# Two more Strassen pairs for the ZA gate blocks of a three-branch mixer, with their gate applied after the read-back

## The chip, the cores and the metric

The kernel runs on one core of one Trainium2 chip. The metric is the device time of one execution in microseconds (us). Three executions of the kernel before took 877.57, 877.92 and 880.95 us; the median is 877.92. One further execution was profiled.

The engines are named as in the profile: PE is TensorE (matmuls), PEld its weight loads, DVE is VectorE, ACT is ScalarE, POOL is GpSimd, SP is the engine from which nearly all DMAs are issued, in order.

## The reference

One decoder layer on a sequence of 1024 tokens with 1024 channels, in float32. Cut to what matters:

```python
mod = c @ w_ada + b_ada
shift, scale, gate = split(mod, 3)
h = rms_norm(x, g_pre) * (1 + scale) + shift
proj = h @ w_in
q_a, kv_c, kv_s, kv_w, g_nsa, z_a, q_b, kv_b, z_b, merge = split(proj)
# mixer A: 8 heads of 64, 2 key/value groups, three branches
o_a = g0 * compressed(q_a) + g1 * selected(q_a) + g2 * windowed(q_a)
y_a = (merge_heads(o_a) * silu(z_a)) @ w_o_nsa
# mixer B: 8 heads, a window of 128 with sinks
o_b = banded_attention(q_b, k_b, v_b, window=128, sinks)
y_b = (merge_heads(o_b) * silu(z_b)) @ w_o_swa
m_a, m_b = split(merge, 2)
y = (sigmoid(m_a) * y_a + sigmoid(m_b) * y_b) @ w_out
out = x + gate * rms_norm(y, g_post)
```

With 16 selected blocks out of 16, the selected branch is full causal attention. `z_a` and `z_b` are 512 columns each, `m_a` and `m_b` 1024 each.

## The kernel before

**Numbers in two halves.** Every float32 operand of a large product is split into a high part (a cast to float32r) and a low part (the rest). A product of a 128-column weight block and a 512-token half is then high x high + high x low + low x high. Over the 8 channel blocks of 128 this makes 24 matmuls of 128x512; over half of them, 12. Splitting a weight quarter (128x512) costs an ACT cast (`wh`) and a POOL subtraction (`wl`), in `split_half` (L180, L183). The input `h` lies in SBUF as `hh` and `hl`, 8 channel blocks x 2 token halves.

**Strassen pairs.** Two weight blocks of 128 columns x two channel halves x two token halves are a 2x2x2 block product. Instead of 8 half products of 12 matmuls each, a pair takes 7 (Winograd's form): two on raw weight quarters of the first block and the raw input half 0 (`raw_products`), three with sums of weights S2, S1, S4, of which two use the input sums T2 and T1 (`middle_products`), and two with S3 on T3 and a quarter of the second block on T4 (`last_products`). The weight sums S1 to S4 are formed on POOL from the four quarters, four additions a pair, and stored to DRAM (`pair_sums`, L852). The input sums T1 to T4 are formed in `input_sums` on POOL and stored; later `set_load` loads one of them over four pairs of `hh` and `hl` tiles whose contents are no longer needed, and `set_form` splits it (an ACT cast L1161, a POOL subtraction L1162, four times each). Partial results go through DRAM: x after the first raw product, then u and e. Before the change the 8 pairs are the 16 merge blocks MA0 to MA7 and MB0 to MB7. The gate blocks ZA0 to ZA3 and ZB0 to ZB3 are plain products of 24 matmuls for each token half.

**Stages.** (1) Norm, conditioning and first projections, to about 95 us. (2) The compression MLP of mixer A, with the gate blocks ZB0 to ZB3, ZA0, ZA1 in between, in 24 steps of 12 matmuls (`z_steps`); `input_sums` hangs on the same steps. (3) Two units of attention of mixer B, one for each key/value group, and then two units of mixer A, each over 8 query tiles of 128. (4) A seam of the last four pairs' last products, then the projection of mixer B by `w_o` with the preparation of `w_out`, that of mixer A, and the output product, itself in seven products.

**What sets the order.** Within the attention, each tile's scores go PE, DVE (masked add with a running minimum, L980), ACT (exponential), DVE (reciprocal), POOL (scaling by the reciprocal and gate, L1002), then PE transposes (L1039), an ACT cast and a DVE subtraction, and PE products with V. Between them stand the projections of the next heads, and pieces of the products of the pairs. In the A units these are written as a `line` of parts: part n of a line stands at the share n / len(line) of the unit's ideal PE time. `pieces` are pumped in that order; a piece may not come before the PE instruction that stands AHEAD of it, and PE work that stands LAG behind it may not come before it. In the B units late gate products run whole at even distances (`Late`, four of them). Weight sums are pieces too, from `late_sums` (B units) and `paced_sums` (A units). Inside these bounds a list scheduler orders each engine's instructions at compile time; each engine then runs its own in order.

**Buffers that matter.** Raw weight quarters have 3 buffers (`wraw`), split ones 6 each. The tag `kt` has 6 tiles of 128x512 and holds partial results, gate temporaries and some keys; `pj` has 2 of 8 PSUM banks. In the last stage the heads are read back through 3 buffers (`t1`).

**The gate of mixer A.** `z_out` makes z * (1 + tanh(z / 2)), twice the SiLU, and stores it to DRAM. `finish` (L1067) loads the gate for a finished query tile as two small DMAs, multiplies the tile by it on POOL, and stores it to `o_dram` (L1070). `heads_out` loads the heads again by halves (L1423), casts on ACT (L1424) and subtracts on DVE (L1425). Before the change heads 4 to 7 (mixer B) are read at the start of the seam, and 0 to 3 after blocks 1, 3, 5, 7 of the projection of mixer B, where `sums_b` also splits the rows of `w_out` (L1495).

## Time and profile before

| what | value |
|---|---|
| median of three executions | 877.92 us |
| profiled execution | 879.03 us |
| its span, first to last instruction | 877.3 us |
| mean granted TensorE clock | 0.993 |
| PE busy | 861.1 us (98%), 4406 matmuls |
| DVE / ACT / POOL busy | 619.0 / 535.1 / 544.0 us |
| DMA | 155.93 MB, mean 178 GB/s |

A row of the groups view names line, engine, operation, output <- inputs, shapes and count, then busy us and mean ns of one, then the engine's idle time before them and what ended most of it. A row of the waits view says who waited for whom: us in total, times, longest us. A row of the stages view has the stretch, its length, and for each engine the busy us with the count of instructions, then the granted clock, the DMA engines' share and GB/s. A row of a timeline has start, length, the instruction, a count where neighbours are merged, and in brackets the idle time before it. A row of the view of one line or tile has the shortest, median and longest duration in ns, then the first and last start.

### The profile page before, as it was taken

To read this page: it belongs to the slowest core of one execution; us is meant where nothing else is said; L and a number is where in the kernel's file an instruction comes from. 1 tells how busy PE (TensorE), PEld (TensorE's weight loads), DVE (VectorE), ACT (ScalarE), POOL (GpSimd) and SP (SyncE) were. 2 spreads that over 40 slices of the span, in tenths; PEclk is the share of its full clock that TensorE was granted. 3 is DMA by queue.
4 is the path that set the end of the run, shared out by engine and by line. 5 is a ranking of instruction groups with operands and counts; after the bars stand their busy time and mean duration, and the time that the engine had idled before them with its cause. 6 is when DMAs were issued, how large, how long until landed. Compare 5 with 4: busy or idle time off the path is not lost.

```text
span 877.3 us, 14795 instructions
## 1 busy us (share of the span) xinstructions
PE 861.1 (98%) x4406; PEld 726.4 (83%) x4406; DVE 619.0 (71%) x1592; ACT 535.1 (61%) x1222; POOL 544.0 (62%) x554
## 2 busy tenths in 40 slices
PE   8999999999999999999999999999999999999996
PEld 6989888888888878888888788888888788887885
DVE  4866677456666677776775677666685399779996
ACT  6466844277768787675776876665565465444341
POOL 2000786568879788987474977664574379646451
PEclk7999999999999999999999999999999999999999
DMA  9874688755545445674225443423554589741333
GB/s 346 287 281 157 223 280 275 255 176 183 150 145 169 136 134 157 213 233 164 75 70 186 124 133 109 145 90 127 196 176 133 180 317 305 283 130 40 108 103 113
DMA packets 95618, 155.93 MB, mean 178 GB/s; under 512 B 11057, under 2 KB 28849, under 8 KB 95538
## 3 DMA queue, kind: packets, MB, share of 16 engines
q1 hardware_dynamic: 89616, 144.84, 50.3%
q10 hardware_dynamic: 5922, 10.14, 3.7%
q8 instruction: 35, 0.57, 0.3%
q14 instruction: 45, 0.37, 0.1%
HBM read 111.43 MB, written 39.85 MB: 172 GB/s over the span
## 4 chain that ended last, share of the span: by engine, by line
PE 94%; DVE 2%; ACT 2%; DMA 1%; issue 1%; POOL 1%; SPq 0%; DVEq 0%; POOLq 0%; ACTq 0%
PE b_pt L1039 8%; PE b_pj L1106 7%; PE b_pj L1112 7%; PE b_pj L1111 7%; PE b_pv L1050 4%; PE b_s L973 4%; PE b_s L970 4%; PE b_pv L1047 4%; PE b_pj L213 3%; PE b_pj L206 3%; PE b_pj L214 3%; PE b_pj L594 1%; PE b_pj L586 1%; PE b_s L593 1%; PE b_s L586 1%; PE b_pj L593 1%
## 5 line engine op out<-in xcount | busy, mean ns | idle before, releaser
L183 POOL TENSOR_TENSOR wl<-wraw,wh 128x512 fp32r<-128x512 f32 x126 | 171.7, 1365 | 103.7 <-ACT wh L180 72.7
L1046 DVE TENSOR_TENSOR pl<-b_pt,ph 128x512 fp32r<-128x512 f32 x162 | 109.7, 686 | 45.1 <-ACT ph L1045 44.6
L1045 ACT CAST ph<-b_pt 128x512 fp32r<-128x512 f32 x162 | 93.1, 584 | 58.2 <-PE b_pt L1039 45.1
L180 ACT CAST wh<-wraw 128x512 fp32r<-128x512 f32 x118 | 72.5, 618 | 60.3 <-PE b_pj L1111 23.6
L993 ACT ACTIVATE ps<-ps,mins 128x257 f32<-128x257 f32 (+9 forms) x128 | 81.1, 635 | 29.2 <-DVE mins L980 27.6
L970 PE MATMUL b_s<-kh,q 128*128 128x256 f32 (+6 forms) x272 | 86.4, 324 | 1.3 <-DVE rr L997 1.1
L973 PE MATMUL b_s<-kl,q 128*128 128x256 f32 (+6 forms) x272 | 83.7, 314 | 0.0
L1002 POOL TENSOR_SCALAR ps<-ps,rr,gates 128x128 f32<-128x128 f32 (+7 forms) x64 | 52.8, 829 | 31.7 <-DVE rr L997 23.7
L1050 PE MATMUL b_pv<-pl,V 128*128 128x512 f32 x162 | 69.0, 426 | 1.2 <-DVE pl L1046 1.0
L1106 PE MATMUL b_pj<-hh,wh 128*128 128x512 f32 x168 | 68.6, 410 | 0.0
L1039 PE MATMUL b_pt<-ident,ps 128*128 128x128 f32 x408 | 67.9, 272 | 0.0
L1047 PE MATMUL b_pv<-ph,V 128*128 128x512 f32 x162 | 66.4, 410 | 1.4 <-ACT ph L1045 1.2
L1112 PE MATMUL b_pj<-hh,wl 128*128 128x512 f32 x168 | 66.4, 395 | 0.0
L1111 PE MATMUL b_pj<-hl,wh 128*128 128x512 f32 x168 | 66.2, 394 | 0.0
L1039 PEld LDWEIGHTS b_pt<-ident,ps 128*128 128x128 f32 x408 | 51.4, 140 | 10.3 <-DVE pl L1018 0.2
L970 PEld LDWEIGHTS b_s<-kh,q 128*128 128x128 f32 x272 | 51.2, 188 | 9.7 <-issue 1.7
L973 PEld LDWEIGHTS b_s<-kl,q 128*128 128x128 f32 x272 | 51.3, 189 | 6.8
L1002 POOL TENSOR_SCALAR pw<-pw,rr,gates 128x640 f32<-128x640 f32 (+4 forms) x64 | 47.6, 747 | 12.5 <-DVE rr L997 9.9
L993 ACT ACTIVATE pw<-pw,mins 128x640 f32<-128x640 f32 (+4 forms) x64 | 44.5, 696 | 13.5 <-DVE mins L980 12.6
L997 DVE RECIPROCAL rr<-sums 128x1 f32<-128x1 f32 x192 | 28.3, 158 | 24.1 <-ACT pw L993 12.6
L206 PE MATMUL b_pj<-hh,wh 128*128 128x512 f32 x112 | 44.6, 398 | 0.0
L213 PE MATMUL b_pj<-hl,wh 128*128 128x512 f32 x112 | 44.3, 396 | 0.0
(460 smaller groups left out, 2588.2 us busy)
## 6 DMA issues: line engine op xcount, KB each, us to landing
wraw<-in_w_blk SPq DMA_DIRECT2D x82, 256.0 KB, 3.3
wraw<-sS SPq DMA_DIRECT2D x32, 256.0 KB, 2.8
r<-in_w_out SPq DMA_DIRECT2D x32, 256.0 KB, 4.2
wa<-in_w_adaT SPq DMA_DIRECT2D x15, 512.0 KB, 5.0
w1raw<-in_w ACTq DMA_DIRECT2D x16, 256.0 KB, 3.2
gr<-in_w_adaT ACTq DMA_DIRECT2D x8, 512.0 KB, 7.1
wraw<-in_w_o SPq DMA_DIRECT2D x16, 256.0 KB, 4.5
t<-od SPq DMA_DIRECT2D x16, 256.0 KB, 4.5
```

What stands on the lines that cost most here:

```text
L183: chain("wl", nc.gpsimd.tensor_tensor(wl, raw, wh.bitcast(F32), ALU.subtract))
L970: ins = nc.tensor.matmul(sp[:, :n_in], lhsT=q, rhs=rh, start=True, stop=False)
L973: nc.tensor.matmul(sp[:, :n_in], lhsT=q, rhs=rl, start=False, stop=True)
L993: nc.scalar.activation(rows[r][:, :on], rows[r][:, :on], AF.Exp, scale=-1.0, bias=last_min[:, r : r + 1], accum_out=sums[:, r : r + 1])
L1002: nc.gpsimd.tensor_scalar(rows[r][:, :off], rows[r][:, :off], rr[:, r : r + 1], gate, ALU.mult, ALU.mult)
L1039: ins = nc.tensor.transpose(t[:, r * P : r * P + P], rows[r][:, off : off + P], ident)
L1046: nc.vector.tensor_tensor(pl, t, ph.bitcast(F32), ALU.subtract)
L1047: ins = nc.tensor.matmul(pv, lhsT=v, rhs=ph, start=(first and n == 0), stop=False)
L1050: nc.tensor.matmul(pv, lhsT=v, rhs=pl, start=False, stop=(last and n == len(todo) - 1))
L1106: ins = nc.tensor.matmul(self.t, lhsT=wh[:, kc, :], rhs=hi, start=(self.first is None and kc == 0), stop=False)
L1111: nc.tensor.matmul(self.t, lhsT=wh[:, kc, :], rhs=lo, start=False, stop=False)
L1112: ins = nc.tensor.matmul(self.t, lhsT=wl[:, kc, :], rhs=hi, start=False, stop=(kc == KH - 1 and self.stop))
```

## The change

- `PAIRS` gets two pairs in front, (ZA0, ZA1) and (ZA2, ZA3), so there are ten. `raw_ends` makes the two evacuations of a raw pair of products; `settle` applies z * (1 + tanh(z / 2)) where the block is a Z, and stores. These and `raw_half_product` serve all places below.
- The raw products are spread out: pairs 0 to 3 (ZA0, ZA2, MA0, MA2) beside the MLP in `z_steps`, after ZB0 to ZB3; pairs 4 to 7 as the four `Late` steps of the B units; pairs 8 and 9 in unit A of group 0.
- The weight sums: pairs 0, 1 and 2, 3 in the two B units, 4 to 7 in unit A of group 0, 8 and 9 in group 1.
- In group 0 the projections of group 1's first half are reordered so that channel half 1 is used up first (`parts` with order (1, 0), and `turned_products` for pair 9, whose sum is added on POOL); T2 and T1 are then loaded and formed there, and the middle products of pairs 0 to 3 run in group 0. Group 1 has those of pairs 4 to 9 and the last products of pairs 0 to 5. The seam keeps the last four pairs.
- `finish` no longer loads or multiplies a gate for mixer A. `heads_out` loads the gate for heads 0 to 3 and multiplies on POOL, 128x512 eight times. Heads 0 and 1 are read during the seam, 2 and 3 after blocks 1 and 3 of the projection of mixer B.

The diff, cut to its core:

```diff
-PLAIN = ["ZA2", "ZA3"]
-PAIRS = [(f"MA{2 * m}", f"MA{2 * m + 1}") for m in range(4)] + [(f"MB{m + 4}", f"MB{m}") for m in range(4)]
+PAIRS = [("ZA0", "ZA1"), ("ZA2", "ZA3")] + [(f"MA{2 * m}", f"MA{2 * m + 1}") for m in range(4)] + [(f"MB{m + 4}", f"MB{m}") for m in range(4)]
-FIRST = 3
+NRAW = (4, 4)
+SUMS = ((0, 1), (2, 3), (4, 5, 6, 7), (8, 9))
+NMID = 4
...
+    def settle(name, half, tile, th=None):
+        if name.startswith("Z"):
+            if th is None:
+                th = kq.tile([P, HS], F32, name="acc", tag="kt", bufs=6)
+            nc.scalar.activation(th, tile, AF.Tanh, scale=0.5)
+            nc.vector.scalar_tensor_tensor(tile, th, 1.0, tile, ALU.add, ALU.mult)
+        store(half_of(name, half), tile)
+
+    def raw_ends(p):
+        c = {}
+        def keep(t):
+            c["x"] = kq.tile([P, HS], F32, name="acc", tag="kt", bufs=6)
+            nc.scalar.copy(c["x"], t)
+            store(x_dram[p], c["x"])
+        def whole_(t):
+            sp = kq.tile([P, HS], F32, name="sp", tag="sp", bufs=1)
+            nc.vector.tensor_tensor(sp, c["x"], t, ALU.add)
+            settle(PAIRS[p][0], 0, sp, c["x"])
+        return keep, whole_
...
-        zs = z_steps([f"Z{m}{b}" for m, b in (("B", 0), ("B", 1), ("B", 2), ("B", 3), ("A", 0), ("A", 1))])
+        zs = z_steps([f"ZB{b}" for b in range(4)], range(NRAW[0]))
...
-        for p in range(2):
+        for p in range(2) if mixer == "B" else ():
             src = spilled[f"Z{mixer}{2 * g + p}"]
...
-        nc.gpsimd.tensor_tensor(ot, ot, zt.rearrange("d r t -> d (r t)"), ALU.mult)
+        if mixer == "B":
+            nc.gpsimd.tensor_tensor(ot, ot, zt.rearrange("d r t -> d (r t)"), ALU.mult)
...
         def whole(self):
-            if not self.w:
-                self.w.extend(load_block(self.name))
-            z_out(self.name, self.half, proj_half(self.w, self.half, lambda: bank("pj")))
+            w = load_block(PAIRS[self.p][0])
+            for j, end in enumerate(raw_ends(self.p)):
+                end(raw_half_product(self.p, j, w[j], lambda: bank("pj"))[0])
...
+    def turned_products(p):
...
+        def keep(t):
+            c["y"] = kq.tile([P, HS], F32, name="acc", tag="kt", bufs=6)
+            nc.scalar.copy(c["y"], t)
+        def whole_(t):
+            x = kq.tile([P, HS], F32, name="acc", tag="kt", bufs=6)
+            nc.scalar.copy(x, t)
+            store(x_dram[p], x)
+            nc.gpsimd.tensor_tensor(c["y"], c["y"], x, ALU.add)
+            store(half_of(a, 0), c["y"])
+        return (Part(Weights(quarter_of(a, 0)), h_set(0, 0), None, whole_),
+                Part(Weights(quarter_of(a, 1)), h_set(1, 0), None, keep))
...
-        late += [Late(name, half, w) for half in range(2)]
+    late = [Late(p) for p in range(NRAW[0], sum(NRAW))]
...
             if u == 2:
-                line = raw_products([0]) + plan_k(g, 1) + plan_q("A", g, 1)
-                line += raw_products([1, 2, 3, 4, 5]) + plan_k(1, 0) + plan_q("A", 1, 0) + raw_products([6, 7])
...
-                behind(line[-1], half_free)
+                rest = range(sum(NRAW), NP)
+                line = raw_products(rest[:1]) + plan_k(g, 1) + plan_q("A", g, 1)
+                q0, q1 = (parts(f"QA1{p}", [0], lambda name, half, t, p=p: q_block("A", 1, p, half, None, t), (1, 0))
+                          for p in range(2))
+                k1 = parts("KA1", [0], lambda name, half, t: k_block([("slc", 1), ("win", 1)], half, None, t), (1, 0))
+                z0, z1 = turned_products(rest[1])
+                line += q0 + [z1, q1[0], k1[0], q1[1], k1[1], z0]
+                behind(k1[0], lambda: set_load("T2", 1, 0))
+                behind(z0, lambda: set_load("T1", 0, 0))
+                mids = [middle_products(p, True) for p in range(NMID)]
+                at0 = len(line)
+                line += [m[0] for m in mids] + sum((m[1:] for m in mids), [])
+                for name, first in (("T2", at0 - 1.2), ("T1", at0 + 2)):
+                    for k in range(KH):
+                        pieces.append((begun + whole[u] * (first + 0.3 * k) / len(line),
+                                       lambda at, name=name, k=k: paced_form(name, k, at)))
+                for n, p in enumerate(SUMS[u]):
+                    for f, share in zip(paced_sums(p), (0.0, 0.05, 0.07, 0.09, 0.11)):
+                        pieces.append((begun + whole[u] * (share + 0.085 * n + 0.05), f))
             else:
                 line = plan_k(g, 1) + plan_q("A", g, 1)
                 behind(line[-1], lambda: set_load("T3", 0, 1))
-                for n, name, k in ((1, "T2", 0), (2, "T2", 1), (3, "T2", 2), (3, "T1", 0),
-                                   (4, "T2", 3), (4, "T1", 1), (5, "T1", 2), (5, "T1", 3)):
-                    ahead_of(line[n], lambda name=name, k=k: set_form(name, (k,)))
-                for p in range(NP):
+                for p in range(NMID, NP):
                     line += middle_products(p)
...
+                for n, p in enumerate(SUMS[u]):
+                    for f, share in zip(paced_sums(p), (0.0, 0.05, 0.07, 0.09, 0.11)):
+                        pieces.append((begun + whole[u] * (share + 0.12 * n + 0.16), f))
                 e = [last_products(p) for p in range(NP - 4)]
                 line += [f[0] for f in e] + [f[1] for f in e]
...
         def heads_out(k):
...
                 nc.sync.dma_start(od, o_dram[k][:, sl])
+                if k < 4:
+                    zt = oh[k][:, sl].bitcast(F32)
+                    nc.sync.dma_start(zt, half_of(f"ZA{k}", half))
+                    nc.gpsimd.tensor_tensor(od, od, zt, ALU.mult)
                 nc.scalar.copy(oh[k][:, sl], od)
...
             early[b, 1], early[b, 0] = e, y
+            if n % 2:
+                heads_out(n // 2)
...
-            if m % 2:
-                heads_out(m // 2)
+            if m in (1, 3):
+                heads_out(2 + m // 2)
             sums_b(m)
```

More of the change, by code (lines that the diff above doesn't have):

```diff
@@ L1088, in __init__ @@
             self.stop = out is not None
+            self.then = None
         def piece(self, k, at, ahead):
@@ L1178, in behind @@
     def behind(part, f):
[L1180 to L1194 removed]
+        part.then = f
     def raw_products(ps_):
```

119 lines of the change are left out of this document (67 added, 52 removed).

## The prediction

> **What bounds the kernel now.** I read the page's first parts, then TensorE's waits, then the busy time stage by stage, then the instruction timelines of the stage after the attention. TensorE (PE in the rows) is busy 98% of the span, in every slice but the first and the last ones, at the full granted clock:
>
> ```profile
> span 877.3 us, 14795 instructions
> PE 861.1 (98%) x4406; PEld 726.4 (83%) x4406; DVE 619.0 (71%) x1592; ACT 535.1 (61%) x1222; POOL 544.0 (62%) x554
> PE   8999999999999999999999999999999999999996
> PEclk7999999999999999999999999999999999999999
> PE 94%; DVE 2%; ACT 2%; DMA 1%; issue 1%; POOL 1%; SPq 0%; DVEq 0%; POOLq 0%; ACTq 0%
> ```
>
> The chain of waits is TensorE for 94%, so a matmul less is time less, unless something else then comes late. The waits of TensorE over the attention on mixer A (310 to 682 us) are all short and of the attention's own kind:
>
> ```profile
> PE b_pv L1047 <- ACT ph L1045: 1.2, 2, 0.9
> PE b_s L970 <- DVE rr L997: 1.1, 1, 1.1
> PE b_pv L1050 <- DVE pl L1046: 1.0, 4, 0.4
> PE b_pt L1039 <- DVE pl L1046: 0.5, 2, 0.3
> ```
>
> By stages (length, then busy us of PE, PEld, DVE, ACT, POOL; the clock; DMA share): first the gate blocks beside the compression MLP, the two B units together from 195 to 310, unit A of group 0, unit A of group 1, the last four pairs' products after the attention, then the projection of mixer B with the preparation of `w_out`, then that of mixer A.
>
> ```profile
> 95.00:195.00 100.00, 100.00 (x515) 84.92 (x514) 63.55 (x119) 48.28 (x99) 73.75 (x59) 1.00 0.78 254
> 195.00:255.00 60.00, 59.71 (x323) 50.27 (x322) 40.33 (x119) 45.72 (x127) 49.35 (x60) 1.00 0.51 155
> 255.00:310.00 55.00, 53.96 (x295) 45.31 (x293) 34.94 (x137) 42.28 (x126) 45.58 (x63) 1.00 0.47 147
> 310.00:497.00 187.00, 185.61 (x1026) 156.75 (x1026) 133.04 (x488) 137.43 (x347) 141.20 (x160) 1.00 0.48 153
> 497.00:682.00 185.00, 183.25 (x983) 154.03 (x984) 127.69 (x401) 114.61 (x262) 118.89 (x127) 1.00 0.43 137
> 682.00:704.00 22.00, 22.00 (x100) 18.20 (x99) 9.26 (x15) 11.31 (x18) 7.70 (x6) 1.00 0.64 219
> 704.00:747.00 43.00, 43.00 (x191) 35.63 (x190) 39.39 (x39) 24.71 (x44) 40.68 (x25) 1.00 0.89 305
> 747.00:790.00 43.00, 43.00 (x191) 35.44 (x191) 33.76 (x41) 19.05 (x33) 22.20 (x16) 1.00 0.59 204
> ```
>
> What the reader should see: TensorE has 0.3 + 1.0 + 1.4 + 1.8 us of idle time in the attention and none from 682 to 790. GpSimd (POOL) comes second, at 83% in the B units (94.9 of 115 us) and at 95% from 704 to 747, where DVE is at 92% and DMA at 0.89 as well. That stage has the least room.
>
> **What the change takes away.** The four ZA blocks cost 4 blocks x 2 halves x 24 matmuls = 192 before. As two pairs they take 2 x 7 products x 12 = 168. So 24 matmuls of 128x512 go. The other counts agree stage by stage: 24 gate steps beside the MLP before and after; four late steps of 24 matmuls in the B units; 28 parts in unit A group 0; in group 1 it is 6 + 8 x 3 + 4 x 2 = 38 parts before and 6 + 6 x 3 + 6 x 2 = 36 after. The saving therefore lands in the last unit. A matmul's price is its step from start to start, not its listed 389 ns, since they overlap:
>
> ```profile
> 687.65 0.40 PE L1439 MATMUL b_s<-hht,wh 128*128 128x512 f32 x1
> ...
> 703.98 0.39 PE L1473 MATMUL b_pt<-oh,wh 128*128 128x512 f32 x1
> ...
> 720.30 0.39 PE L1473 MATMUL b_pj<-oh,wh 128*128 128x512 f32 x1
> ```
>
> Between the first two rows lie 72 matmuls, so 16.33 / 72 = 0.227 us each, and 24 x 0.227 = **5.44 us saved**. Every one stands on the chain. Nothing hides it.
>
> **What it adds beside TensorE.** The prices:
>
> ```profile
> L183 POOL TENSOR_TENSOR wl<-wraw,wh 128x512 fp32r<-128x512 f32 x126 | 171.7, 1365 | 103.7 <-ACT wh L180 72.7
> L852 POOL TENSOR_TENSOR ps<-ps 128x512 f32<-128x512 f32 x12 | 15.5, 1295 | 0.9 <-PE b_pt L1039 0.7
> L1067 POOL TENSOR_TENSOR ot<-ot,zt 64x512 f32<-64x512 f32 x16 | 20.6, 1285 | 5.0 <-DVE ot L1066 3.2 <-PE b_pj L1442 1.0 <-DVE rr L997 0.8
> L1162 POOL TENSOR_TENSOR hlt<-hlt,hht 128x512 fp32r<-128x512 f32 x16 | 20.6, 1299 | 4.0 <-ACT hht L1161 4.0
> L1495 POOL TENSOR_TENSOR hlw<-r,hhw 128x512 fp32r<-128x512 f32 x16 | 26.5, 1689 | 7.3 <-ACT hhw L1495 7.3
> ```
>
> Beside the MLP: four pairs' weights serve 12 matmuls a quarter where two blocks' served 24, so 4 quarters more, 4 x 1.365 = 5.5 us of POOL on 73.75 of 100, and some 2 MB more of DMA on a share of 0.78. The 26 us that POOL has free cover it; bare, it would cost its 5.5 us; nothing can be gained, since TensorE does not idle there. I take 0.
>
> B units: 4 quarters more (late products) and one pair of sums more (four of 1.295): 5.2 + 5.2 = 10.4 us of POOL on 94.9 of 115. Free time there halves, 20.1 to 9.7 us. Queued behind on POOL are the softmax scalings that the transposes wait for. TensorE's idle time there is 0.29 + 1.04 = 1.33 us. The bounds: -1.3, if another order of the late products fills it, and the 10.4 us themselves. I take **+0.8**, nearer to the covered end, because POOL still has idle time.
>
> Units A: 16 multiplications with their 32 small gate loads go (L1067, 20.6 us of POOL). In group 0, 8 of them and 4 sums go and the forming of T2 and T1 (8 operations) and one addition come, 3 fewer operations; in group 1, 8 multiplications, 8 formings and 2 weights go and 8 sums come, 10 fewer. Each set of input sums now has more than a part (187 / 28 = 6.7 us) between its loads and its forming, and its forming begins more than a part ahead of its first use. Before, the loads came at the end of group 0 and the formings around the change of units, where TensorE waits:
>
> ```profile
> L1154 SPq DMA_DIRECT2D hlt<-T2d x4: 319/320/374, 465.8 to 469.7; - x4
> L1162 POOL TENSOR_TENSOR hlt<-hlt,hht x16: 1261/1298/1322, 478.0 to 646.7; 128x512 fp32r<-128x512 f32 x16
> 497.92 0.41 PE L970 MATMUL b_s<-kh,q 128*128 128x384 f32 x1 [1.11 <-DVE rr L997]
> L1210 DVE TENSOR_TENSOR sp<-acc,b_pj 128x512 f32<-128x512 f32 x8 | 5.5, 681 | 3.0 <-PE b_pj L1112 3.0
> ```
>
> TensorE idles 1.39 + 1.75 us in the two units. Bounds: -3.1 (all of it goes) and, were a set late, the part of 6.7. I take **-0.5**. DVE gets seven additions of 0.68 us (L1210) a pair, 9.5 us on 261 of 372, which has room.
>
> After the attention: 8 multiplications of 128x512 and 8 loads of 256 KB (2 MB) come into 690 to 747, and half of the read-backs move ahead of the B projection. What they run into:
>
> ```profile
> 697.76 1.29 POOL L183 TENSOR_TENSOR wl<-wraw,wh 128x512 fp32r<-128x512 f32 x1 [2.64 <-ACT wh L180]
> 706.32 9.80 POOL L1495 TENSOR_TENSOR hlw<-r,hhw 128x512 fp32r<-128x512 f32 x6 [7.27 <-ACT hhw L1495]
> 716.08 5.15 POOL L183 TENSOR_TENSOR wl<-wraw,wh 128x512 fp32r<-128x512 f32 x3
> 721.19 8.12 POOL L1495 TENSOR_TENSOR hlw<-r,hhw 128x512 fp32r<-128x512 f32 x5
> SPq L164 <- POOL wl L183: 19.2, 14, 8.6
> SPq L1423 <- DVE ol L1425: 2.5, 4, 0.8
> SPq L1070 <- POOL ot L1067: 1.9, 1, 1.9
> ```
>
> The three weights split at 716 to 721 are the fourth to sixth of the B projection. The fourth is done at about 717.8 (a third of 5.15 us) and its first matmul is the one at 720.30, so the narrowest lead is 2.5 us. The multiplications cost 8 x 1.295 = 10.4 to 8 x 1.689 = 13.5 us. Ahead of them POOL is idle for 7.27 us; but the loads of the heads wait in SP's queue for the three buffers that DVE frees (L1423 behind L1425), and behind them in that queue stand the next weights and the rows of `w_out`. In return the last heads no longer pass through POOL, so the store that SP waits for (L1070) and all behind it come 1.29 us earlier. The 2 MB at the stage's 305 GB/s are 6.9 us of DMA, for which 0.36 x 22 + 0.11 x 43 = 12.7 us are free from 682 to 747. Bounds: 0 (TensorE has no idle time here to lose, and what does not fit before 706 is put off to 747 to 790, where POOL has 20.8 us free), and all eight at a mean of 1.55 less the lead, 12.4 - 2.5 = 9.9. Two of them ahead of the fourth weight are 3.1 us against a lead of 2.5, three are 4.7; less the 1.29, that is 0 to 0.9. Since SP's queue may hold something else back too, I take **+1.2**.
>
> How often POOL and DVE get in each other's way here shows in the subtraction that splits the read heads, 0.68 us alone:
>
> ```profile
> L1425 DVE TENSOR_TENSOR ol<-t,oh x16: 681/1182/1781, 694.6 to 737.2; 128x512 fp32r<-128x512 f32 x16
> ```
>
> Its median is 1.18 and its longest 1.78 us while POOL works. [...]
>
> **The sum.** -5.44 + 0.8 - 0.5 + 1.2 = -3.94 us. The profiled execution took 879.03 us, 1.7 more than its span; the median of the three runs is 877.92, and I apply the difference to that: **874.0 us**, 0.45% less. What a measurement here can tell from no change is about 0.5%, 4.4 us, so faster begins under 873.5 and slower above 882.3.
>
> **Rivals.** (1) The covers hold everywhere and the last unit's saving comes whole: -5.44, and -0.5 in the A units, **872.0**. For it: the waits of matmuls quoted above name neither POOL nor a DMA. Against: the 2.5 us lead. (2) In the preparation of `w_out`, POOL's multiplications are queued ahead of the weights of the B projection: POOL, at 40.68 of 43 us, becomes the bound, and the price is 9.9 us: 877.92 - 5.44 + 9.9 = **882.4, slower**. It decides from about two multiplications (2.5 us) before the fourth weight on; to be slower than before, 5.44 + 2.5 = 7.9 us, some five of them, must stand there. Against it: POOL's 7.27 idle us before 706 and the 20.8 after 747. (3) POOL binds the B units: half of the 10.4 us arrives at TensorE, **877.7**. Against it: 9.7 us stay free. (4) A set is late: one part's time, 6.7 us, is waited out, **879.2**; the gap of more than a part speaks against it. That the change does not do what it says is not to be feared: 24 matmuls fewer can be counted in the code.
>
> **Chances.** Forecast (872.9 to 876.5) 0.48; rival 1 0.27; rival 2 0.08; rival 3 0.11; rival 4 0.06. Faster: rival 1 and a third of the forecast's cases, 0.44. Slower: most of rival 2 and the worst of rival 4, 0.07. Same: 0.49. The range goes from 870.0 (rival 1 with most of the idle time of units A gone) to 879.5, which takes in rivals 3 and 4 and the lighter half of rival 2. The forecast's own range is 872.9 to 876.5.
>
> **What would show it.** TensorE should count 4382 instructions, with the last unit shorter by about 5 us than its 185 and the others as long as before. Right in the B units: POOL near 105 of 115 us and TensorE's idle time up by less than 1. Right after the attention: no wait of a PE load on POOL's weights over 1 us, and the B projection again 43 us long. Wrong would be a row of TensorE waiting for `wl` or for `ol`, a projection of B that takes 45 us or more, idle time before the first T2 product of group 0, or a total idle time of TensorE before 650 us that changes by over 3 us.

## The result: 1.2% slower, with the saving there and two new losses

The changed kernel takes 888.61 us (median of 6 runs, 887.35 to 891.51); the kernel before, beside it, 878.43 us (6 runs). The ratio is 1.012, 95% interval 1.0107 to 1.0133. The forecast was 874.0 us with a range to 879.5.

The first parts of the page after:

```profile
span 888.8 us, 14799 instructions
PE 862.2 (97%) x4382; PEld 723.0 (81%) x4382; DVE 627.9 (71%) x1605; ACT 540.0 (61%) x1231; POOL 552.8 (62%) x561
PE   9999999799999999999999999999999999899996
```

TensorE counts 4382 instructions, the 24 fewer that were forecast (the second row is the share of the span in which TensorE is busy, in 40 slices, in tenths). But two slices that were full are no longer: the eighth (around 170 us) and the one around 790 us.

To find where the time went I cut the span at the first start of five groups of matmuls: gate steps beside the MLP, first product with V of mixer B, seam, projection of B, output product. Three of the rows, from the view of one line, first of the kernel before, then of the changed one; the two numbers ahead of the semicolon are the first and the last start:

```profile
L1047 PE MATMUL b_pv<-ph,V x162: 388/393/508, 192.2 to 680.7; 128*128 128x512 f32 x162
L1473 PE MATMUL b_pt<-oh,wh x32: 389/389/389, 704.0 to 782.2; 128*128 128x512 f32 x32
L1603 PE MATMUL b_pt<-hhw,wh x20: 389/389/393, 786.5 to 854.0; 128*128 128x512 f32 x20
```

```profile
L1112 PE MATMUL b_pv<-ph,V x162: 388/395/507, 197.0 to 681.1; 128*128 128x512 f32 x162
L1553 PE MATMUL b_pt<-oh,wh x32: 389/389/629, 704.4 to 793.1; 128*128 128x512 f32 x32
L1683 PE MATMUL b_pt<-hhw,wh x20: 388/389/390, 798.4 to 865.9; 128*128 128x512 f32 x20
```

| from one first start to the next | before | after | difference |
|---|---|---|---|
| start to the gate steps | 94.0 | 92.7 | -1.3 |
| beside the MLP, to the first product with V | 98.2 | 104.3 | +6.1 |
| attention, to the seam | 489.7 | 485.3 | -4.4 |
| seam | 22.1 | 22.1 | 0 |
| projections, to the output product | 82.5 | 94.0 | +11.5 |
| output product, to the end of the span | 90.8 | 90.4 | -0.4 |

(The gate steps start at 94.0 and 92.7, the seam at 681.9 and 682.3.) The differences add up to the 11.5 us between the spans. The change does not touch the first row, and kernels with the same code there start these steps anywhere from 92.3 to 94.3 us. So the attention is shorter by most of the 5.44 us, and 17.6 us are lost in two places. TensorE's waits in these two, from 150 to 200 us and from 700 to 800 us after, name them:

```profile
PE b_pt L851 <- DVE he L843: 3.1, 1, 3.1
PE b_s L1035 <- ACT acc L603: 1.8, 1, 1.8
```

```profile
PE b_pt L1555 <- POOL wl L184: 2.7, 2, 1.8
PE b_pt L1553 <- ACT oh L1502: 1.7, 1, 1.7
PE b_pt L1554 <- DVE ol L1503: 1.6, 1, 1.6
PE b_pt L1553 <- ACT wh L181: 1.4, 1, 1.4
PE b_pj L1553 <- ACT oh L1502: 0.7, 1, 0.7
```

The kernel before has no wait at all in these stretches of TensorE. The waits are 4.9 of 6.1 us and 8.1 of 11.5 us; part of the rest is told in the last section: in each of the two stretches the granted clock was 0.50 for 3.4 us after a stall, from 173.9 to 177.2 and from 791.7 to 795.0, which by the estimate there costs about 1.6 us each time. The two B units and the projection of B after, with the columns of the prediction's table:

```profile
195.00:255.00 60.00, 60.00 (x328) 50.87 (x328) 38.58 (x114) 46.46 (x125) 51.90 (x63) 1.00 0.59 184
255.00:310.00 55.00, 54.35 (x300) 46.28 (x299) 36.03 (x130) 42.90 (x124) 50.85 (x64) 1.00 0.66 201
704.00:747.00 43.00, 40.71 (x179) 33.08 (x178) 32.12 (x35) 22.14 (x40) 34.86 (x24) 1.00 0.87 303
```

GpSimd is not busier in the projection (34.86 us where it was 40.68): it is not a lack of GpSimd's time on average, but of its time at a moment.

### The profile page after: what moved, and what is told of

Read it like the earlier page. It is cut to its first block, busy times and chain, and to the rows that moved or that the text cites. A ratio compares the mean times of both kernels' runs of the same rounds, so it can differ in the third digit from the quotient of the medians.

```text
span 888.8 us, 14799 instructions
## 1 busy us (share of the span) xinstructions
PE 862.2 (97%) x4382; PEld 723.0 (81%) x4382; DVE 627.9 (71%) x1605; ACT 540.0 (61%) x1231; POOL 552.8 (62%) x561
## 5 line engine op out<-in xcount | busy, mean ns | idle before, releaser
L184 POOL TENSOR_TENSOR wl<-wraw,wh 128x512 fp32r<-128x512 f32 x132 | 179.3, 1362 | 117.7 <-ACT wh L181 86.0
L1172 PE MATMUL b_pj<-hht,wh 128*128 128x512 f32 x128 | 52.7, 412 | 0.0
L1172 PE MATMUL b_pj<-hh,wh 128*128 128x512 f32 x128 | 52.5, 412 | 0.0
L1178 PE MATMUL b_pj<-hh,wl 128*128 128x512 f32 x128 | 50.6, 396 | 0.0
L1178 PE MATMUL b_pj<-hht,wl 128*128 128x512 f32 x128 | 50.5, 395 | 0.0
L1177 PE MATMUL b_pj<-hlt,wh 128*128 128x512 f32 x128 | 50.4, 394 | 0.1
L1177 PE MATMUL b_pj<-hl,wh 128*128 128x512 f32 x128 | 50.4, 393 | 0.0
```

Of the source, the lines that this page charges most:

```text
L184: chain("wl", nc.gpsimd.tensor_tensor(wl, raw, wh.bitcast(F32), ALU.subtract))
L1172: ins = nc.tensor.matmul(self.t, lhsT=wh[:, kc, :], rhs=hi, start=(self.first is None and kc == 0), stop=False)
L1177: nc.tensor.matmul(self.t, lhsT=wh[:, kc, :], rhs=lo, start=False, stop=False)
L1178: ins = nc.tensor.matmul(self.t, lhsT=wl[:, kc, :], rhs=hi, start=False, stop=(kc == KH - 1 and self.stop))
```

## The experiments

My theory after the two traces: (a) in the projection the gate multiplications stand in GpSimd's order in front of weight differences, which is the prediction's rival 2; (b) beside the MLP a tile of the raw products comes free only with a store that is late. The rivals: the gate loads, not the products, do (a); the added work itself, on whichever engine and with whichever tiles, does (b).

All kernels in one table; stage lengths as above, from one profiled execution each, and "MLP" is the stage beside it. The ratio is to the kernel before on the same chip.

| kernel | MLP | attention | projections | median us | ratio, 95% interval |
|---|---|---|---|---|---|
| before | 98.2 | 489.7 | 82.5 | 878.43 | 1 |
| changed | 104.3 | 485.3 | 94.0 | 888.61 | 1.012 (1.0107 to 1.0133) |
| no_gate | 103.8 | 485.0 | 84.5 | 881.36 | 1.0032 (1.0013 to 1.0052) |
| gate_load_only | 104.1 | 485.2 | 83.1 | 878.98 | 1.0005 (0.999 to 1.0019) |
| own_buffers | 101.8 | 486.2 | 90.3 | 885.23 | 1.0072 (1.0047 to 1.0097) |
| gate_dve | 101.9 | 484.1 | 88.8 | 883.46 | 1.0055 (1.0037 to 1.0073) |
| own_tile | 105.9 | 485.6 | 92.0 | 888.37 | 1.0116 (1.0096 to 1.0135) |
| z_store_act | 100.7 | 485.7 | 91.5 | 883.61 | 1.0055 (1.0034 to 1.0075) |
| z_free | 103.2 | 485.5 | 92.4 | 888.1 | 1.0106 (1.0091 to 1.0121) |
| z_free_act | 101.8 | 484.3 | 91.5 | 884.12 | 1.0066 (1.0052 to 1.008) |
| z_act_dve | 101.7 | 485.8 | 88.6 | 882.84 | 1.0052 (1.003 to 1.0075) |
| early_gate | 104.1 | 488.7 | 84.1 | 886.25 | 1.0093 (1.008 to 1.0106) |
| z_early | 101.0 | 488.2 | 84.1 | 882.84 | 1.0066 (1.0042 to 1.009) |
| z_kts | 110.7 | 485.0 | 91.5 | 895.88 | 1.0206 (1.0184 to 1.0229) |
| z_kts_act | 109.9 | 484.1 | 92.7 | 893.08 | 1.0172 (1.0155 to 1.0189) |
| kts_early | 110.1 | 485.6 | 85.3 | 888.47 | 1.0125 (1.0108 to 1.0142) |
| m_first | 104.2 | 486.4 | 92.4 | 890.6 | 1.0141 (1.0124 to 1.0157) |
| m_first_act | 100.0 | 486.1 | 92.6 | 884.28 | 1.0063 (1.0043 to 1.0083) |
| m_act_early | 98.0 | 486.0 | 86.3 | 878.82 | 1.0012 (1.0001 to 1.0024) |
| m_act_early_dve | 99.2 | 484.3 | 84.3 | 875.09 | 0.9957 (0.994 to 0.9974) |

Kernels with the same code in a stage differ there by up to 2.5 us (the projections of the changed kernel's code: 91.5 to 94.0; the stage beside the MLP: 101.8 to 104.3). That is the resolution of the stage columns. Part of this spread goes with the clock of the last section: beside the MLP, the changed kernel (104.3) has 3.4 us at half clock, and gate_dve (101.9) has a clock of 1.00 from 95 to 195 us; in the projections, the changed kernel (94.0) has another 3.4 us at half clock, and z_store_act, z_free_act, m_first and m_first_act (91.5 to 92.6) have 1.00 from 704 to 790 us.

### The projections: is it the gate's products?

no_gate leaves out the gate of mixer A altogether, so its output lacks the SiLU of z_a. gate_load_only loads the gates but does not multiply, so it lacks it too.

```diff
# no_gate
-                if k < 4:
-                    zt = oh[k][:, sl].bitcast(F32)
-                    nc.sync.dma_start(zt, half_of(f"ZA{k}", half))
-                    nc.gpsimd.tensor_tensor(od, od, zt, ALU.mult)
# gate_load_only: the last of these lines alone goes
```

> Changed kernel with the gate of heads 0 to 3 left out in the read-back: neither the eight loads of it nor the eight multiplications (the output then lacks the factor SiLU(z_a)); the places of the read-backs stay as changed. Theory (POOL link): the multiplication stands between the load and the ACT cast, ACT waits for it in order (11.8 us in seven waits), and the weights' casts behind it come late; without it the projections of the two mixers lose 10 to 11 us and the kernel takes 877 to 879 us. Rival (loads): the 2 MB of loads do it; also 877 to 879 us here. Rival (places): it is the moved read-backs; then 886 to 889 us.

> Changed kernel with the eight gate loads of the read-back kept and the eight multiplications left out (the output lacks the factor SiLU(z_a)). Theory (POOL link): nearly as without both, 877 to 880 us. Rival (loads): as the changed kernel, 886 to 889 us.

The stage falls from 94.0 to 84.5 and 83.1 us, near the 82.5 of before. In the medians the products cost 888.61 - 878.98 = 9.6 us, and their 2 MB of loads nothing that can be seen. (Measured against no_gate, which missed its 877 to 879 us and whose ten runs spread from 877.17 to 884.9, it is 7.3 us. That the kernel with more work is the faster of the two by 2.4 us shows how far medians of such variants can be trusted.) What the eight products do is in GpSimd's timeline, of the changed kernel:

```profile
719.34 1.30 POOL L1575 TENSOR_TENSOR hlw<-r,hhw 128x512 fp32r<-128x512 f32 x1 [1.34 <-ACT hhw L1575]
720.60 1.28 POOL L1501 TENSOR_TENSOR t<-t,oh 128x512 f32<-128x512 f32 x1
721.85 4.68 POOL L184 TENSOR_TENSOR wl<-wraw,wh 128x512 fp32r<-128x512 f32 x3
...
747.66 1.29 POOL L1501 TENSOR_TENSOR t<-t,oh 128x512 f32<-128x512 f32 x1
...
751.87 3.41 POOL L1501 TENSOR_TENSOR t<-t,oh 128x512 f32<-128x512 f32 x2
755.24 5.11 POOL L184 TENSOR_TENSOR wl<-wraw,wh 128x512 fp32r<-128x512 f32 x3
```

and in the waits of all engines between 700 and 800:

```profile
DVE ol L1503 <- ACT oh L1502: 15.1, 8, 3.7
ACT oh L1502 <- POOL t L1501: 11.8, 7, 2.6
```

From 719 us on GpSimd runs from one instruction into the next. A head half goes through it in turn with weight differences and rows of `w_out`; ScalarE stands for its product (7 times), VectorE for ScalarE (8 times), TensorE for both. The three weights at 721.85 come behind a product, and those at 755.24 behind two.

own_buffers takes away the three read-back buffers as a cause: heads 0 to 3 are read into the storage of `ya`, which is not in use yet.

```diff
-                od = tmp("t1", 3)
+                od = ya[1][:, k, sl] if k < 4 else tmp("t1", 3)
```

> Changed kernel in which heads 0 to 3 are read back into parts of the projection's result tile that are still free, instead of through the three shared buffers; gate and multiplication stay. Theory (late data): the multiplications come late, from 720 us on, because their tiles wait for buffers that DVE frees; with buffers of their own those of heads 0 and 1 run in POOL's idle time before 706 us and the kernel takes 880 to 884 us. Rival (POOL's room): POOL lacks 12 us in this stage wherever the tiles lie; then 886 to 889 us.

885.23 us in all is between the two: the buffers seem to be a part of it (3.4 us in the medians), the smaller one; the stage alone, 90.3 us, is too close to the 91.5 of the changed code to tell. The four products of heads 0 and 1 do run early now, from 701.19 to 712.40 us, in GpSimd's idle time. TensorE waits for weights instead:

```profile
PE b_pj L1555 <- ACT wh L181: 2.2, 1, 2.2
...
PE b_pj L1557 <- POOL wl L184: 0.9, 1, 0.9
```

The stage can be cut after its first 192 matmuls, as many as the projection of B has (8 blocks x 2 halves x 12). Before, the two parts take 43.5 and 39.0 us, in the changed kernel 46.4 and 47.6, in own_buffers 51.3 (4.3 us of it waits of TensorE) and 39.0. So in the changed kernel most of the loss is in the projection of A, which waits for its gated heads; where the heads come early, all of it is in the projection of B, which waits for its weights.

gate_dve puts the products on VectorE.

```diff
-                    nc.gpsimd.tensor_tensor(od, od, zt, ALU.mult)
+                    nc.vector.tensor_tensor(od, od, zt, ALU.mult)
```

> The changed kernel, but the gate of A is multiplied by VectorE instead of GpSimd when the head outputs are read back; GpSimd keeps the differences of the weights. The theory that the loss in the output projection is GpSimd's order (a multiplication stands in front of weight differences, and head outputs behind these) expects the projection's stage at 84 to 87 us instead of 94.0 and 879.5 to 881.5 us in all, a little more than without the multiplication (83.1 us) for 16 more products on VectorE. The rival, that one more link between read-back and the rounded head outputs costs this on whichever engine it is done, expects 92 to 96 us for the stage and 887 to 890 us.

It comes between again, 88.8 us (84 to 87 expected) and 883.46: the waits for weights go, but VectorE becomes the one that is late:

```profile
PE b_pj L1554 <- DVE ol L1503: 1.7, 1, 1.7
PE b_pj L1553 <- ACT oh L1502: 1.3, 1, 1.3
```

So it is not one engine's order alone. Both engines had hardly any free time there already. That can be read in the kernel before, in a window narrower than the prediction's (columns PE, PEld, DVE, ACT, POOL):

```profile
715.00:745.00 30.00, 30.00 (x134) 24.82 (x133) 29.65 (x29) 15.41 (x28) 30.00 (x19) 1.00 0.85 286
```

30.00 of 30 us on GpSimd and 29.65 on VectorE. early_gate tests this by place: the same eight products on the same engine, six of them moved to the last unit of A, on tiles read back from DRAM and written there again.

```diff
+    def gate_early(k, half):
+        ...
+            od, zt = fresh(o_dram[k][:, sl]), fresh(half_of(f"ZA{k}", half))
+            nc.gpsimd.tensor_tensor(od, od, zt, ALU.mult)
+            store(o_dram[k][:, sl], od)
...
-                if k < 4:
+                if k < 4 and (k, half) not in gated_early:
```

> The changed kernel, but six of the eight gate multiplications of A (both halves of heads 0 and 1, the first halves of heads 2 and 3, whose gates and outputs are complete by then) are done by GpSimd in the last unit of A, on tiles read from the spills and written back; at the read-back only the second halves of heads 2 and 3 are multiplied. The work is the same and adds six stores and six reads; only its place differs: from 560 to 680 us GpSimd is busy about half the time, from 715 to 760 all of it. The theory that the loss of 11.4 us is the crowding of GpSimd and VectorE at the read-back expects a quarter of it to be left: output projection's stage 83.5 to 87 us, 879.5 to 882.5 us in all. If even two multiplications ahead of the weights hold the head outputs as long, 90 to 93 us and 885 to 888 us. If the attention pays for the six in its place, its part grows by 3 us or more.

The stage is 84.1 us, as the crowding theory expects, but the attention takes 488.7 instead of 485.3 us, so the kernel gains 2.4 of the 9.6. Of the three outcomes written down, the first for the stage and the third for the attention came true: place decides, and this place had a price of its own. A full GpSimd alone did not stop TensorE: from 715 to 745 us it is busy 30.00 of 30 us in early_gate too, and TensorE does not wait there once. So it is not a full engine in itself that costs, but operands that come late through it. In z_early (below), which has the same six products, a last product's evacuation waits 3.95 us for its load at 632 us, and TensorE 1.9 us behind it, where in z_free_act, without them, it is 2.08 and 0.8; in early_gate itself TensorE waits 1.8 us for such an evacuation. How much of the 3.4 us this makes up was not measured by itself.

### Beside the MLP: what is late?

The timeline of SyncE and ScalarE in the changed kernel:

```profile
150.39 0.32 SPq L578 DMA_DIRECT2D sp_ZB<-sp  x1
159.01 0.33 SPq L165 DMA_DIRECT2D wraw<-in_w_blk  x1
159.43 0.38 SPq L581 DMA_DIRECT2D xd<-acc  x1
```

```profile
150.46 0.59 ACT L603 COPY acc<-b_s 128x512 f32<-128x512 f32 x1
162.67 0.63 ACT L593 ACTIVATE acc<-sp 128x512 f32<-128x512 f32 x1 [6.23 <-DMA xd<-acc]
166.83 0.38 ACT L842 ACTIVATE he<-b_pt 126x256 f32<-126x256 f32 x1 [1.73 <-DMA wraw<-in_w_blk]
```

The first raw product of ZA0 is copied at 150.46. Its store stands behind a weight load in SyncE's queue, and that load waits for a buffer that GpSimd has to free; it is issued at 159.43. The tanh of `settle` overwrites that tile, so it waits until 162.67, and behind it on ScalarE stands everything else, the MLP's own step at 166.83 too (the profile puts the last 1.73 us before that one down to a weight load). Behind this step, and behind a sum on VectorE that waits 0.74 us for a store, TensorE waits 3.1 us. The queue stood as long in the kernel before; the first row below is its wait, the second that of the changed kernel (140 to 170 us):

```profile
SPq L164 <- POOL wl L183: 14.3, 4, 8.1
```

```profile
SPq L165 <- POOL wl L184: 14.8, 5, 8.2
```

There no wait of ScalarE names a store, from 145 to 180 us.

own_tile gives the tanh a tile of its own.

```diff
-            settle(PAIRS[p][0], 0, sp, c["x"])
+            settle(PAIRS[p][0], 0, sp)
```

> Changed kernel with one edit: the tanh of a Z pair's first block goes into a tile of its own instead of over the tile of the first product. Theory (tile): ACT's tanh waits in its in-order queue until the DMA that stores that tile has landed, 6.2 and 4.1 us, and the tanh of the MLP and the evacuation of a score bank behind it make TensorE idle 3.15 + 1.79 us and bring the half-clock stretch after it; the stage beside the MLP then ends some 6 us earlier and the kernel takes 882 to 883 us, with no clock below 1.00 between 150 and 200 us. Rival (weights): the four extra weight quarters and their POOL subtractions are what is late; then the time stays at 888 to 889 us.

888.37 us: nothing gained. The wait for the store of x is gone, and the next store is waited for in its place, on VectorE, with the MLP's step right behind it:

```profile
170.91 0.69 DVE L608 TENSOR_TENSOR sp<-acc,b_pj 128x512 f32<-128x512 f32 x1 [8.76 <-DMA sp_ZA<-sp]
171.51 0.41 DVE L843 SCALAR_TENSOR_TENSOR he<-he,b_pt 126x256 f32<-126x256 f32 x1
```

The sum of a pair goes into `sp`, a single tile, which is free when the last sum's store has landed. So the theory of one tile fell, and the theory of the queue took its place: z_store_act leaves every tile as it is and issues these stores from ScalarE. TensorE, VectorE and GpSimd keep the order of the changed kernel.

```diff
-        nc.sync.dma_start(dst, tile)
+        (nc.scalar if hold[0] is None else nc.sync).dma_start(dst, tile)
```

> The changed kernel, but while the raw products of the Z pairs are made (before the attention is paced) their stores are issued by ScalarE instead of SyncE; the orders of TensorE, VectorE and GpSimd stay as in the changed kernel, and no tile or buffer is another. In own_tile the wait on the store of x went away and one on the store of the single sp tile took its place, so the theory is now that of the queue: any tile of these products comes free only with its store, and the store stands in SyncE's queue behind weight loads that wait for GpSimd. It expects the first weigh matmul of B at about 191 to 193 us instead of 197.0, no half clock around 175, and a time of 882.5 us (881.5 to 884). The rival, that the extra tanh, addition and product themselves come too late on ScalarE and VectorE whatever releases their tiles, expects 887.5 to 889.5; six more issues on ScalarE would then add up to 1 us.

883.61 us, 100.7 us for the stage: 3.6 of its 6.1 us are back, less than expected by about 1 us, and a stretch at half clock, which was not to come, is still there (the clock is 0.89 from 165 to 175 us and 0.94 from 175 to 185, together 3.4 us at half). What is left is the landing: the store issued at 166.06 (first row, ScalarE) holds the sum at 170.66 and the MLP's h1T behind it:

```profile
166.06 0.33 ACTq L581 DMA_DIRECT2D sp_ZA<-sp  x1
```

```profile
170.66 0.69 DVE L608 TENSOR_TENSOR sp<-acc,b_pj 128x512 f32<-128x512 f32 x1 [4.61 <-DMA sp_ZA<-sp]
...
171.34 0.41 DVE L854 TENSOR_SCALAR h1T<-b_pt 128x252 f32<-128x252 f32 x1
```

z_free and z_free_act were to give room instead of, or beside, early stores: the sum and the tanh in tiles of the tag `kt`, with six.

```diff
-            sp = kq.tile([P, HS], F32, name="sp", tag="sp", bufs=1)
+            tag, bufs = ("kt", 6) if hold[0] is None else ("sp", 1)
+            sp = kq.tile([P, HS], F32, name="sp", tag=tag, bufs=bufs)
...
-            settle(PAIRS[p][0], 0, sp, c["x"])
+            settle(PAIRS[p][0], 0, sp)
```

> The changed kernel, but the raw Z products evacuate into tiles of the six-buffer tag: a tanh tile of its own, and the sum not in the single sp tile; the stores stay in SyncE's queue. If a number of buffers is enough to cover a late queue: 882.5 us (881.5 to 884), as with the stores moved. If the queue is late by more than six buffers cover (a pair now takes three of them, and the queue stood for 8.6 us while TensorE makes a pair's two products in 5.5 us), the wait only moves to a later tile: 884 to 888.

> The changed kernel with both edits of the stage beside the MLP: the raw Z products go into tiles of the six-buffer tag (own tanh tile, sum not in the single sp tile), and their stores are issued by ScalarE. In z_store_act the second sum still waited 4.61 us for the first one's store, issued at 166.06 and landed at about 170.6; in z_free the tiles were apart but their stores late. If late stores and too few tiles are the whole cause, neither wait is left: first weigh matmul of B 98.2 to 99.5 us after the first matmul beside the MLP (before 98.2, changed 104.3, z_store_act 100.7, z_free 103.2), no half clock, and 881.5 to 883.5 us. If the extra work on ScalarE and VectorE costs something by itself, the distance stays at 100.5 to 102 us and the time at 883.5 to 885.5 us.

They gave no room. z_free is at 888.1, and in z_free_act the sum waits as it did:

```profile
171.85 0.69 DVE L609 TENSOR_TENSOR sp<-acc,b_pj 128x512 f32<-128x512 f32 x1 [4.91 <-DMA sp_ZA<-sp]
```

I had counted the six tiles and not who else holds them then (the tag also holds keys and gate temporaries). z_kts and z_kts_act took another tag, with eight (z_kts_act with the stores from ScalarE):

```diff
+                sp, th = (kq.tile([P, P + HS], F32, name="sp", tag="kts", bufs=8)[:, :HS] for _ in range(2))
```

> The changed kernel, but the sum and the tanh of a raw Z product beside the MLP go into tiles of an eight-buffer tag, which the MLP's second weights have nearly left by then; the stores stay in SyncE's queue. If the number of tiles is the cause, whatever the queue: no sum waits for the store of another, 98.2 to 99.5 us from the first matmul beside the MLP to the first weigh matmul of B, 881.5 to 883.5 us. If late stores of x alone hold ScalarE, 101 to 103 us and 885 to 887.5 us.

> As z_kts, with the stores issued by ScalarE. If tiles and late stores together are the whole cause: 98.2 to 99.5 us for the stage, no half clock near 175, 881.5 to 883 us. If ScalarE's order does it, in which the copies of the products stand behind casts of weights whose loads are late (the copy at 167.10 in z_free_act came 4.8 us after its product), 100 to 101.5 us and 883 to 885 us, whatever the tiles.

Both are far off, 895.88 and 893.08 us, because the MLP's second weights still needed that tag; in z_kts TensorE stands for them:

```profile
PE b_pt L831 <- ACT w L826: 5.3, 2, 3.3
```

They tell nothing about the tiles of the Z products, and more room for these was not tried in another way. The last pair of runs shortens the chain instead: pairs without a tanh (MA) are made beside the MLP, the two Z pairs in the units of B; m_first with the stores on SyncE, m_first_act from ScalarE.

```diff
+RAW = (2, 3, 4, 5, 0, 1, 6, 7)
...
-        zs = z_steps([f"ZB{b}" for b in range(4)], range(NRAW[0]))
+        zs = z_steps([f"ZB{b}" for b in range(4)], RAW[: NRAW[0]])
-    late = [Late(p) for p in range(NRAW[0], sum(NRAW))]
+    late = [Late(p) for p in RAW[NRAW[0] :]]
```

> The changed kernel, but the four pairs whose raw products are made beside the MLP are MA pairs (no tanh, no product), and the two Z pairs go into the units of B; stores as in the changed kernel, by SyncE. If the loss beside the MLP is the chain sum, tanh, product, store through one tile, shorter by the two middle steps: 99.5 to 101.5 us from the first matmul beside the MLP to the first weigh matmul of B (before 98.2, changed 104.3) and 883.5 to 886 us. If only the late stores count, which stay: 103 to 105 us and 887 to 889.5 us.

> m_first with these stores issued by ScalarE, so each is issued within about 1 us of its sum. The chain of a pair is then sum 0.7, issue 0.4 and landing 3 to 5 us, about the 5.5 us of TensorE in which the next pair's products are made: 98.2 to 99.5 us for the stage and 881.5 to 883.5 us. If casts of late weights on ScalarE hold the copies all the same: 100 to 101.5 us and 883 to 885 us. If the Z pairs cost in the units of B what they cost here, that part grows by 1 us or more.

Without the tanh, but with late stores, the stage is 104.2 us, as with it: the added tanh and product are not the cause. With early stores it is 100.0 us, in the range of the second outcome written down, and 98.0 and 99.2 us in the two kernels below that have the same stage. So the late stores are what costs 4 to 6 us, the clock's drop after the stalls included (from 95 to 195 us the clock is 0.97 in m_first, about 6 us at half, and 1.00 in the three others). One rival is left, that SyncE, rid of the stores, fetches the weights earlier. The traces speak against it: ScalarE's casts of the next weights, which start from 161.76 to 173.82 us in m_first, start from 163.85 to 175.44 in m_first_act, later and not earlier. The Z pairs cost at most about 1 us in the units of B (attention 486.1 and 486.4 us, for 485.3).

### Both repairs together

z_act_dve is z_store_act with gate_dve; z_early is z_free_act with early_gate; kts_early is z_kts_act with four of the six early products put behind the last products of the unit; m_act_early is m_first_act with these.

```diff
-EARLY_MID = ((12, 0, 0), (16, 0, 1), (22, 2, 0))
-EARLY_LAST = (((2, 0), 1, 1), ((2, 1), 1, 0), ((4, 1), 3, 0))
+EARLY_MID = ((10, 0, 0), (15, 0, 1))
+EARLY_END = ((1, 1), (1, 0), (2, 0), (3, 0))
```

> The changed kernel with both edits: the raw Z products' stores issued by ScalarE, and the gate of A multiplied by VectorE. If the two losses stand apart in time, as the stage table says (6.1 us beside the MLP, 11.4 us in the output projection), what the two edits regain adds up: 873.5 to 876 us, below the kernel before. If the output projection's loss is tied to any work of the gate, 881 to 884 us; if the stage beside the MLP keeps its loss, 879 to 882 us.

> The edits of z_free_act and early_gate together. If the losses are these two and stand apart: about 1 us left beside the MLP, 2 us left in the output projection, and the attention's gain of 4.4 us: 875 to 878 us, at or below the kernel before. If the regained time is shared or a third place pays, 880 us or more.

> z_kts_act, and six of the eight gate multiplications of A done before the read-back: two early in the last unit of A, four behind its last products, where no tile of these is waiting. If the three places are understood: at most 1 us lost beside the MLP, the attention 4 to 5 us shorter than before, 84 us for the output projection's stage (before 82.5), together 875 to 877.5 us. If the four at the end delay the seam or the tiles of the next pool, the seam takes 24 us or more (before 22.1) and the time is 878.5 to 882 us.

> m_first_act, and six of the eight gate multiplications of A done in the last unit of A as in kts_early. Summing the stages: 0.5 to 1 us lost beside the MLP, 4.1 us gained in the attention (485.6 for 489.7), 2.8 us lost in the output projection (85.3 for 82.5): 877 to 878 us, level with the kernel before. If the multiplications of the gate end up in the way of the Z pairs' own steps: 880 us or more.

z_act_dve was to be 873.5 to 876 and is 882.84: the two stages came back only by 2.6 and 5.4 us, so what adds up is less than expected. z_early keeps the attention's price (488.2), and with it takes 882.84 us where 875 to 878 were to come. kts_early, slow beside the MLP for the reason of z_kts, shows that the four products at the end cost the attention nothing (485.6) and the seam nothing (22.1). m_act_early has both and comes to 878.82, the level of the kernel before, as its stages sum up to. Two products are still at the read-back; m_act_early_dve moves these two to VectorE, with TensorE's order unchanged.

> m_act_early, but the two gate multiplications of A that are left at the read-back (second halves of heads 2 and 3) are done by VectorE; TensorE's order is the same. If GpSimd's continuous queue (busy from 706.4 to 747.5 us without a break in m_act_early) is what the two lengthen: 83 to 84.5 us for the output projection's stage instead of 86.3, and 875.5 to 877.5 us, a little below the kernel before. If the gap left is GpSimd's wl at 778.5, which stands behind a difference that waited 7.6 us for a product, it stays: 85.5 to 87 us and 878 to 880 us.

875.09 us, ratio 0.9957 (0.994 to 0.9974): 0.4% faster than the kernel before and about 1.5% faster than the changed one. The interval does not reach 1, though 0.4% is less than the 0.5% that the prediction counted as faster, and this is the best of 18 variants. m_act_early is 3.7 us slower in the medians; the stage that the last edit touches accounts for 2.0 of them (84.3 for 86.3, as expected). Its page and its waits of TensorE from 90 to 200 and 690 to 800 us:

```profile
span 874.2 us, 14816 instructions
```

```profile
PE b_s L1038 <- ACT acc L606: 1.7, 1, 1.7
```

```profile
PE b_pt L1574 <- POOL wl L187: 1.1, 1, 1.1
PE b_pj L1574 <- POOL wl L187: 0.3, 1, 0.3
```

The waits of 4.9 and 8.1 us have become 1.7 and 1.4.

## Why the prediction was wrong, step by step

**The saving: right.** 24 matmuls fewer, and the attention 4.4 us shorter; -5.44 + 0.8 - 0.5 is -5.1. What I took for the units of B and A is 0.7 us off, within its bounds. The saving lies in the last unit, as forecast: at its start the changed kernel's products with V are 5.2 us behind those of the kernel before, at its end 0.4 us. Rival 3 did not come: GpSimd has 102.75 of 115 us in the units of B (near 105 was forecast) and TensorE idles 0.65 us there, not more than before. Rival 4 did not come: no wait of TensorE in the A units names a set.

**Beside the MLP: "I take 0" was wrong, by 6.1 us.** The step priced GpSimd's four weight quarters (5.5 us) and named GpSimd's 26 free us as the cover. GpSimd was not the matter. The step left out what the raw products do after the matmuls: a copy, a sum and two stores for each 24 matmuls where one store had been, and a tanh that writes over a tile whose store has not left. Of these the late stores are what costs; without the tanh the stage is as long. The kernel before shows SyncE standing up to 8.1 us behind GpSimd's weights in that stretch, and I did not look at that queue there, though the step moved stores behind it and made engines wait for them. That TensorE did not idle there was read as a sign of room; it only says that there was no wait yet.

**After the attention: "I take +1.2" was wrong, by 6 to 10 us.** Measured are 9.6 us in the medians against gate_load_only, 7.3 against no_gate, and 7.0 to 10.9 in the stage. Rival 2 (0.08) had a price of 9.9 us, but that it fits is partly luck, because rival 2 put all of it in front of the weights of the projection of B. There TensorE waits 1.4 us for `wh` at 723 and 0.9 us for `wl` at 741, and that part is 2.9 us longer. The other 8.6 of the 11.5 us are in the projection of A. There TensorE waits for the gated heads themselves, these two times and 0.7 us once more, then 1.8 us for a weight at 789, with a stretch at half clock behind it (0.50 from 791.7 to 795.0):

```profile
755.98 0.50 PE L1553 MATMUL b_pt<-oh,wh 128*128 128x512 f32 x1 [1.67 <-ACT oh L1502]
759.26 0.50 PE L1554 MATMUL b_pt<-ol,wh 128*128 128x512 f32 x1 [1.62 <-DVE ol L1503]
```

So the step priced only what a product does to the weights behind it. That each head half now passes one more engine before its cast and its difference, in a stretch where each of these waits its turn, was in no term. own_buffers shows the case that rival 2 described, with the heads early and the loss in front of the weights.

What also failed is the argument against rival 2. GpSimd's 7.27 idle us before 706 were of no use: that is a wait for rows of `w_out`, and no product of the gate ran before 720.60. The gates were loaded from 694.1 us on, but the heads go through three buffers behind the eight halves of mixer B, and the ninth head load is issued at 709.44; with storage of their own the products ran from 701.19. That "what does not fit before 706 is put off to 747 to 790" failed too: in the trace GpSimd runs the products where they stand in its order, among the weights at 720 to 764. The window of 704 to 747 us averaged GpSimd to 95%; inside it, from 715 to 745, there was no free time on GpSimd and 0.35 us on VectorE. With that row, rival 2 would have deserved far more than 0.08. Its total of 882.4 was still 6.2 us short, about what the MLP's stage lost.

Longer subtractions on VectorE did not do it: the median of the split of the heads is 1104 ns after, for 1182 before, and VectorE is busy 32.12 us instead of 39.39 from 704 to 747.

```profile
L1503 DVE TENSOR_TENSOR ol<-t,oh x16: 683/1104/1745, 694.7 to 766.1; 128x512 fp32r<-128x512 f32 x16
```

**What would show it: right as a list.** Of the signs named as wrong, three came: rows of TensorE waiting for `wl` and `ol`, a projection of B of 46.4 us, and idle time before 650 us that changed by more than 3 us. (In the chances, 0.27 and a third of 0.48 make 0.43 for faster, not 0.44.)

## What to carry to other kernels

Before work is put into a stage that is full on average, cut the window down to the stretch where the neighbours run from one instruction into the next; free time before or after it is of use only if the operands are there and the written order lets it. When a product's end is moved, follow each tile to the store that frees it, and that store through its queue: here ScalarE, which waited 6.23 us for a store, inherited what SyncE's queue waited for, up to 8.2 us for GpSimd. A loss on a crowded stretch was had back here mostly by moving the work to where its inputs were first complete (94.0 to 84.1 us for six of eight products), and only in part by giving it to another engine there (88.8).

## What was not expected of the hardware

After some stalls of TensorE the granted clock fell to half, for 3.4 us each time in the changed kernel; in m_first, where it is 0.97 from 95 to 195 us, that makes an estimated 6 us. In the changed kernel this happens after the stalls that end at 169 and 173 us:

```profile
170.00:173.80 3.80, 2.00 (x11) 1.35 (x10) 1.36 (x3) 2.14 (x4) 1.29 (x2) 1.00 0.93 336
173.90:177.20 3.30, 3.30 (x11) 2.53 (x9) 1.61 (x3) 1.10 (x2) 2.41 (x2) 0.50 0.85 274
```

```profile
174.12 0.63 PE L625 MATMUL b_pj<-hl,wh 128*128 128x512 f32 x1
174.54 0.63 PE L626 MATMUL b_pj<-hh,wl 128*128 128x512 f32 x1
...
178.44 0.39 PE L618 MATMUL b_pj<-hh,wh 128*128 128x512 f32 x1
178.67 0.40 PE L625 MATMUL b_pj<-hl,wh 128*128 128x512 f32 x1
```

The step from matmul to matmul is 0.42 us in it and 0.23 after it, so by an estimate from these two a stretch of 3.4 us costs about 1.6 us; there is another after the stall at 789 us, 0.50 from 791.7 to 795.0. That is 1.6 us on top of the 4.9 and of the 8.1 us of waits. The kernel before has none between 18 and 874 us (1.00), m_act_early_dve none from 95 to 195 us, nor from 704 to 799 (1.00 in both), despite a stall of 1.7 us in the first. The length of the stalls does not tell which of them do it: in z_store_act, where TensorE idles 1.67 us in all from 95 to 195 us, the clock dropped (0.89 from 165 to 175); in gate_dve, where it idles 3.95 us in that stretch, it stayed at 1.00, as it did after two stalls of 1.7 and 1.6 us within 5 us, at 754 and 758 in the changed kernel. Which stalls do it stays open.
